# Attention in one encoder kernel: the work of later heads is queued, turn by turn, behind the turn's exponential and negated maximum

## The chip, the cores and the metric

The kernel runs on one core of a Trainium2 chip. A core has engines that each work through a queue of their own and wait for one another by semaphores: TensorE (PE in the profile, with its weight loads as PEld) for matmuls, VectorE (DVE), ScalarE (ACT), GpSimd (POOL) and SyncE (SP, which here only issues DMAs). The metric is device time in microseconds of one execution; a median of several runs stands for a kernel.

## The reference

The program is an encoder trunk of two residual layers on 512 tokens of width 1024, all in float32. Layer 0 mixes tokens with a gated linear attention, layer 1 with softmax attention; each is followed by a gated MLP with a short convolution. The change lies in layer 1's attention alone, which computes

```python
q = apply_rope(rmsnorm(q, q_norm)...)   # 8 heads of 128
k = apply_rope(rmsnorm(k, k_norm)...)   # 2 heads; query heads 0-3 use the first, 4-7 the second
...
s = einsum('bkgqd,bksd->bkgqs', q_blk, k) * scale    # per block of 128 queries
p = softmax(s, axis=-1)
o = einsum('bkgqs,bksd->bkgqd', p, v)
...
return o @ w_out
```

With 512 tokens and blocks of 128 queries there are 4 blocks for each of 8 heads, so 32 blocks. Each has a score tile of 128 queries by 512 keys.

## The kernel before

Products run on TensorE in a reduced float format. To keep precision each operand is split in a high part and a low rest, and a product is three matmuls (`mm3`, lines 253 to 255): high by high, high by low, low by high. So every weight half of 128x1024 has to be made into a pair, `wh` and `wl`. In most of the kernel ACT makes `wh` by a rounding copy (L140) and DVE makes `wl` by a subtraction (L141). In the attention layer DVE is relieved: ACT makes `wh` (L123) and a negated copy in `wl` (L124), and POOL issues a DMA that adds the raw weight into `wl` (L133, called from `flush`). `W.half` returns a pair that has been made and makes the one after it, so a pair is made one call ahead. `wh` and `wl` have three buffers each, the raw weights two of 1 MB, which SP loads.

The attention layer first projects keys, the first pair of query heads and the values. Then comes the loop over turns t = 0 to 37, which the change touches. One turn does, in the order in which the program is traced:

- `scores` of block t: three matmuls into a bank "s" (two banks), the row maximum on DVE (L753), the negated and scaled maximum nb on DVE (L754), the exponential p with its row sum on ACT (L756)
- what the `plan` has for the turn: steps of generators that do work of later heads
- `turn` of block t - 4: four transposes of p on TensorE (L774) into a bank "pt" (two banks), a rounding copy on ACT (L777) and its rest on DVE (L778)
- `shares` of block t: the reciprocal of the sum (L761) and p times it (L762), on DVE
- `mix` of block t - 6, for two blocks at a time: twelve matmuls of the transposed probabilities with the values into bank "po", and for every fourth block the split of the head's result on ACT and DVE (L678, L679).

The plan has two kinds of generators. Three are the query projections `qpair` of the pairs of heads 1 to 3, of 27 steps each: 8 steps of matmuls into a bank A and 8 into a bank B (the three matmuls of one of eight slices each), then squares of A and B on ACT (L642, L643), their sum (L644), four products with the rotary tables on DVE (`turned`, L652), the sums of squares over a head on TensorE (`hs`, L626, into a "pt" bank) with its scale on DVE and POOL (L628, L193, L197, L633), the rotation's sums on POOL (L671, L672), and two splits of the finished q on ACT and DVE (L678, L679). `Q_STEPS` and `Q_READY` say how many steps fall into which turn: pair 1 has its matmuls in turns 0 to 3 and the rest in turns 4 to 8, pair 2 in turns 4 to 10 and 11 to 16, pair 3 in turns 11 to 19 and 20 to 24. Scores of pair i begin with block 8i. The fourth generator is the output projection `out_steps`, with six matmuls a step (L308) in the turns of `O_STEPS`, from turn 22 on; what is left of it follows the loop. The calls of `W.half` fall into turns 0, 2, 4, 7, 11, 15, 22 and 29, and then 32 and 36.

The order on each engine is not the traced order. A scheduler at compile time plays the program through and gives each engine its next instruction from those that are ready, with earlier traced ones first. So an instruction of a generator whose operands are ready early can stand on its engine well ahead of the turn that it was traced in. What follows from data (a value, a buffer to be freed) is kept by semaphores.

Of the kernel before, what the change touches and what calls it, by code (L numbers as in the profile page):

```python
# [11 lines left out]
AF = mybir.ActivationFunctionType  # L12
ALU = mybir.AluOpType
# [33 lines left out]
def hybrid_encoder_kernel(  # L47
# [21 lines left out]
    pe, act, dve, pool, sync = nc.tensor, nc.scalar, nc.vector, nc.gpsimd, nc.sync  # L69
# [14 lines left out]
    def bank(tag, n):  # L84
        return pp.tile([P, S], F32, tag=tag, bufs=PS[tag], name=nm(n))
# [7 lines left out]
    def tmp(tag, n, w=S):  # L93
        return sp.tile([P, w], F32, tag=tag, bufs={"u": 4, "t": 6, "sq": 3}[tag], name=nm(n))

    def tiny(w, n, tag="tiny"):
        return sp.tile([P, 8], F32, tag=tag, bufs={"tiny": 36, "tiny2": 4}[tag], name=nm(n))[:, :w]
# [153 lines left out]
    def mm3(ps, wh, wl, mh, ml, start, stop):  # L251

        mm(ps, wh, mh, start=start, stop=False)  # L253
        mm(ps, wh, ml, start=False, stop=False)  # L254
        mm(ps, wl, mh, start=False, stop=stop)  # L255
# [356 lines left out]
    def attention(norm, nxt):  # L612
# [89 lines left out]
        def qpair(i, tag="acc"):  # L702
            ys, sc = yield from roped(1 + i, PC_QK, HD ** -0.5, "qsc", tag)
            for e in range(2):
                yield
                t = big(F32R, "q")
                split(ys[e], t)
                heads[2 * i + e] = (t, sc, e)
# [35 lines left out]
        def scores(h, j):  # L744

            qt, sc, e = heads[h]
            kt = kk[h // 4]
            js = slice(j * P, (j + 1) * P)
            s = bank("s", "s")
            mm3(s, qt[:, js], qt[:, S + j * P : S + (j + 1) * P], kt[:, :S], kt[:, S:], True, True)  # L750
            scj = sc[:, 2 * j + e : 2 * j + e + 1]
            mx, nb, sm, rc = (tiny(1, n) for n in ("mx", "nb", "sm", "rc"))
            dve.reduce_max(mx, s, axis=mybir.AxisListType.X)  # L753
            dve.tensor_scalar(nb, mx, scj, -1.0, ALU.mult, ALU.mult)  # L754
            p = tmp("t", "p")
            act.activation(p, s, AF.Exp, scale=scj, bias=nb, accum_out=sm)  # L756
            probs[h, j] = (p, sm, rc)

        def shares(h, j):
            p, sm, rc = probs[h, j]  # L760
            dve.reciprocal(rc, sm)  # L761
            dve.tensor_scalar(p, p, rc, None, ALU.mult)  # L762
            probs[h, j] = p

        def turn(h, j):

            hf, i = divmod(j, 2)
            if i == 0:
                pts[h, hf] = tuple(big(F32R, n).rearrange("p (k q) -> p k q", q=256) for n in ("pth", "ptl"))
            ph3, pl3 = pts[h, hf]  # L770
            p = probs.pop((h, j))
            tp = bank("pt", "pt")
            for k in range(NT):
                pe.transpose(tp[:, k * P : (k + 1) * P], p[:, k * P : (k + 1) * P], ident)  # L774
            isl = slice(i * P, (i + 1) * P)
            tp3 = tp.rearrange("p (k q) -> p k q", q=P)
            act.activation(ph3[:, :, isl], tp3, AF.Copy)  # L777
            dve.tensor_tensor(pl3[:, :, isl], tp3, ph3[:, :, isl].bitcast(F32), ALU.subtract)  # L778

        def mix(h, hf):  # L780
            ph3, pl3 = pts.pop((h, hf))
            vo = (h // 4) * HD
            if hf == 0:
                pos[h] = bank("po", "po")
            dst = pos[h][:, hf * 256 : (hf + 1) * 256]
            for k in range(NT):
                vsl = slice(k * 256 + vo, k * 256 + vo + HD)
                mm3(dst, vh[:, vsl], vl[:, vsl], ph3[:, k, :], pl3[:, k, :], k == 0, k == NT - 1)
            if hf == 1:
                t = big(F32R, "oT") if h < 4 else pair("xhl", 8, F32R, "oT")  # L790
                split(pos[h], t)
                oh[h] = (t[:, :S], t[:, S:])

        LAG, LAG2 = LAGS
        blocks = [(h, j) for h in range(QH) for j in range(NT)]
        osteps = out_steps(w_aout, oh, nxt)
        plan = collections.defaultdict(list)
        for i in range(1, QH // 2):
            g = qpair(i)
# [3 lines left out]
        for t in O_STEPS:  # L803
            plan[t].append(osteps)
        for t in range(len(blocks) + LAG2):
            if t < len(blocks):
                scores(*blocks[t])
            for g in plan[t]:
                next(g, None)
            if LAG <= t < len(blocks) + LAG:  # L810
                turn(*blocks[t - LAG])
            if t < len(blocks):
                shares(*blocks[t])
            if t >= LAG2:
                h, j = blocks[t - LAG2]
                if j % 2 == 1:
                    mix(h, j // 2)
# [3 lines left out]
    cw = gla(norms[0], norms[1])  # L821
    ffn(0, norms[1], cw, norms[2])
    attention(norms[2], norms[3])
    ffn(1, norms[3], cw, None)

# [80 lines left out]
```

## Time and profile before

| what | value |
|---|---|
| runs | 1138.2, 1138.27, 1138.65 us; median 1138.27 |
| profiled execution | 1138.36 us, of which the profile's span is 1136.6 |
| TensorE busy | 1128.9 us, 99% of the span, 5280 matmuls |
| DVE, ACT, POOL busy | 688.0, 481.5, 84.4 us |
| granted TensorE clock | 0.999 of full speed |

The span goes from the first to the last instruction of the profile. A row of a timeline gives the start in us from the span's start, the duration in us, the engine, the line, the operation, what it writes and reads with shapes, and in brackets the idle time of the engine before it and what ended it. Matmuls overlap, and the ends of their records are modelled: the step from one matmul's start to the next is what it costs, not the length of its record. In a row of waits stand the total in us, how often, and the longest.

### The profile page before, as it was taken

Reading aid. Unit: us, or ns where it says so; the run is one execution under the profiler, and the core shown is the slowest. Engines: PE = TensorE matmul, PEld = TensorE weight load, DVE = VectorE, ACT = ScalarE, POOL = GpSimd, SP = SyncE. Lnnn points to the kernel's source line nnn. Section 1 sums busy time; section 2 is a strip of 40 time slices with the busy share of each in tenths; the row PEclk is TensorE's granted clock in tenths of the full one; section 3 lists DMA queues with packets and bytes.
Section 4 is the critical chain, followed back from the end, with each engine's and each line's share of the span. In section 5 each row is a group of like instructions: output and inputs, shape, how many; then the busy total and the mean of one; then the engine's idle time right before and its main releaser. Section 6 shows DMA issues by size and latency. Waiting matters only on the chain. (4 is left out here: it accounts for less than half of the span.)

```text
span 1136.6 us, 13040 instructions
## 1 busy us (share of the span) xinstructions
PE 1128.9 (99%) x5280; PEld 941.8 (83%) x5280; DVE 688.0 (61%) x997; ACT 481.5 (42%) x691; POOL 84.4 (7%) x73
## 2 busy tenths in 40 slices
PE   9999999999999999999999999999999999999998
PEld 7788888888888888888888888888888888888887
DVE  5677653567776777633325689756777777762221
ACT  6465233444444444432234666644444444441210
POOL 0214110000000000000004333000000000000000
PEclk9999999999999999999999999999999999999999
DMA  6322211232322323223257632222232322323320
GB/s 229 137 86 74 78 71 38 74 106 80 111 80 106 111 75 111 91 95 112 76 151 182 149 75 74 56 75 94 92 111 75 111 100 86 111 80 124 130 93 19
DMA packets 19980, 111.66 MB, mean 98 GB/s; under 512 B 2384, under 2 KB 3024, under 8 KB 8400
## 3 DMA queue, kind: packets, MB, share of 16 engines
q1 hardware_dynamic: 17328, 102.29, 25.7%
q0 software_dynamic: 2304, 8.39, 3.9%
q8 instruction: 41, 0.67, 0.2%
q10 hardware_dynamic: 288, 0.15, 0.0%
q14 instruction: 19, 0.16, 0.0%
HBM read 100.34 MB, written 2.10 MB: 90 GB/s over the span
## 5 line engine op out<-in xcount | busy, mean ns | idle before, releaser
L140 ACT ACTIVATE wh<-raw 128x1024 fp32r<-128x1024 f32 x164 | 173.0, 1055 | 339.6 <-PE up L254 132.5
L141 DVE TENSOR_TENSOR wl<-raw,wh 128x1024 fp32r<-128x1024 f32 x164 | 203.8, 1243 | 149.9 <-ACT wh L140 149.5
L253 PE MATMUL up<-xhl,wh 128*128 128x512 f32 x704 | 274.3, 390 | 0.0
L255 PE MATMUL up<-xhl,wl 128*128 128x512 f32 x704 | 273.9, 389 | 0.0
L254 PE MATMUL up<-xhl,wh 128*128 128x512 f32 x704 | 273.9, 389 | 0.0
L255 PEld LDWEIGHTS up<-xhl,wl 128*128 128x128 f32 x704 | 132.2, 188 | 27.6
L254 PEld LDWEIGHTS up<-xhl,wh 128*128 128x128 f32 x704 | 132.2, 188 | 27.3
L253 PEld LDWEIGHTS up<-xhl,wh 128*128 128x128 f32 x704 | 132.2, 188 | 27.2
L253 PE MATMUL dn<-gu,wh 128*128 128x512 f32 x352 | 136.9, 389 | 0.0
L254 PE MATMUL dn<-gu,wh 128*128 128x512 f32 x352 | 136.9, 389 | 0.0
L255 PE MATMUL dn<-gu,wl 128*128 128x512 f32 x352 | 136.9, 389 | 0.0
L579 DVE TENSOR_TENSOR u<-up,R 128x512 f32<-128x512 f32 x88 | 60.3, 687 | 52.7 <-PE up L255 52.6
L581 ACT ACTIVATE y<-u,cw 128x512 f32<-128x512 f32 x88 | 71.2, 811 | 21.6 <-DVE u L579 21.6
L254 PEld LDWEIGHTS dn<-gu,wh 128*128 128x128 f32 x352 | 66.1, 188 | 13.8
L253 PEld LDWEIGHTS dn<-gu,wh 128*128 128x128 f32 x352 | 66.1, 188 | 13.7
L255 PEld LDWEIGHTS dn<-gu,wl 128*128 128x128 f32 x352 | 66.1, 188 | 13.6
L308 PE MATMUL op<-oT,wh 128*128 128x512 f32 x256 | 70.6, 394 | 0.0
L583 DVE SCALAR_TENSOR_TENSOR y<-u,cw,y 128x511 f32<-128x511 f32 x88 | 65.9, 751 | 2.9
L582 DVE SCALAR_TENSOR_TENSOR y<-u,cw,y 128x511 f32<-128x511 f32 x88 | 65.5, 746 | 0.6 <-ACT y L581 0.6
L585 ACT ACTIVATE y<-y 128x512 f32<-128x512 f32 x44 | 27.9, 634 | 87.8 <-DVE y L583 87.7
L308 PEld LDWEIGHTS op<-oT,wh 128*128 128x128 f32 x256 | 47.2, 188 | 9.8 <-ACT oT L539 0.3
L282 PE MATMUL vg<-wl,xhl 128*128 128x512 f32 x128 | 49.9, 390 | 0.2 <-DVE wl L141 0.2
(191 smaller groups left out, 1504.8 us busy)
## 6 DMA issues: line engine op xcount, KB each, us to landing
raw<-in_w_up_dram SPq DMA_DIRECT2D x44, 1024.0 KB, 4.7
raw<-in_w_down_dram SPq DMA_DIRECT2D x22, 1024.0 KB, 4.7
wl<-raw POOLq DMA_DIRECT2D x16, 512.0 KB, 4.6
raw<-in_w_vg_dram SPq DMA_DIRECT2D x6, 1024.0 KB, 4.8
raw<-in_w_akq_dram SPq DMA_DIRECT2D x5, 1024.0 KB, 5.2
raw<-in_w_kq_dram SPq DMA_DIRECT2D x4, 1024.0 KB, 4.7
raw<-in_w_gout_dram SPq DMA_DIRECT2D x4, 1024.0 KB, 4.8
raw<-in_w_aout_dram SPq DMA_DIRECT2D x4, 1024.0 KB, 4.8
```

The lines of the kernel that those rows point to most:

```text
L140: act.activation(hi[:, sl], r[:, sl], AF.Copy)
L141: dve.tensor_tensor(lo[:, sl], r[:, sl], hi[:, sl].bitcast(F32), ALU.subtract)
L253: mm(ps, wh, mh, start=start, stop=False)
L254: mm(ps, wh, ml, start=False, stop=False)
L255: mm(ps, wl, mh, start=False, stop=stop)
L282: mm(ps[j][:, :width], xh, wl[:, sl], start=False, stop=False)
L308: mm(pss[ng][n], wt[:, sl], mv, start=k == 0 and i == 0, stop=k == KC - 1 and i == 2)
L579: dve.tensor_tensor(u, ps, norm.R, ALU.mult)
L581: act.activation(y, u, AF.Identity, scale=w(1), bias=w(3))
L582: dve.scalar_tensor_tensor(y[:, 1:], u[:, : S - 1], w(0), y[:, 1:], ALU.mult, ALU.add)
L583: dve.scalar_tensor_tensor(y[:, : S - 1], u[:, 1:], w(2), y[:, : S - 1], ALU.mult, ALU.add)
L585: act.activation(res[1], res[1], AF.Silu)
```

## The change

`scores` now returns two instructions: nb's (the last that it puts on DVE) and the exponential (on ACT). The loop opens `tc.issue_after` for both around the turn's planned steps. Within the block, each instruction that is traced on the engine of the given one gets an ordering edge to it: the scheduler may not place it on that engine before the given one. It is an edge of issue order on one engine alone, with no semaphore and no wait for the given instruction's end. So in turn t planned instructions on DVE stand behind nb of block t, planned instructions on ACT behind exponential t. Instructions of TensorE, POOL and SP get no edge. `turn`, `shares` and `mix` stay outside the block; from turn 32 on there are no scores and no edges.

```diff
             dve.reduce_max(mx, s, axis=mybir.AxisListType.X)
-            dve.tensor_scalar(nb, mx, scj, -1.0, ALU.mult, ALU.mult)
+            last = dve.tensor_scalar(nb, mx, scj, -1.0, ALU.mult, ALU.mult)
             p = tmp("t", "p")
-            act.activation(p, s, AF.Exp, scale=scj, bias=nb, accum_out=sm)
             probs[h, j] = (p, sm, rc)
+            return last, act.activation(p, s, AF.Exp, scale=scj, bias=nb, accum_out=sm)
...
         for t in range(len(blocks) + LAG2):
-            if t < len(blocks):
-                scores(*blocks[t])
-            for g in plan[t]:
-                next(g, None)
+            with ExitStack() as behind:
+                if t < len(blocks):
+                    for i in scores(*blocks[t]):
+                        behind.enter_context(tc.issue_after(i.ins))
+                for g in plan[t]:
+                    next(g, None)
             if LAG <= t < len(blocks) + LAG:
```

## The prediction

> **What bounds the kernel now.** I read the page first: engine totals, then the chain that ended last.
>
> ```profile
> span 1136.6 us, 13040 instructions
> PE 1128.9 (99%) x5280; PEld 941.8 (83%) x5280; DVE 688.0 (61%) x997; ACT 481.5 (42%) x691; POOL 84.4 (7%) x73
> ...
> PE 37%; ACT 0%; POOL 0%; DVE 0%; DVEq 0%; issue 0%
> ```
>
> TensorE is busy for 1128.9 of 1136.6 us and is the only engine on the chain with a share. So a stretch in which TensorE finds nothing to do is added to the time whole, and no other engine's saving counts unless it feeds TensorE. Next the windows: the loop over the 32 blocks, from the first scores at 629 to the last at 727, and its 18 us tail. The columns are busy times of PE, weight load, DVE, ACT and POOL, then clock, DMA share and GB/s.
>
> ```profile
> 629.00:727.00 98.00, 96.92 (x558) 82.12 (x558) 78.34 (x189) 66.29 (x125) 29.75 (x25) 1.00 0.39 93
> 727.00:745.00 18.00, 18.00 (x112) 15.63 (x111) 8.41 (x17) 6.42 (x12) 0.00 (x0) 1.00 0.12 52
> ```
>
> The loop holds 98.00 - 96.92 = 1.08 us of idle TensorE. No more than that can be gained there, but for waits that overlapping records hide. The waits of the stretch 620 to 750 (total, times, longest):
>
> ```profile
> ACT p L756 <- DVE nb L754: 17.0, 17, 2.6
> PEld s L253 <- ACT p L756: 2.3, 5, 1.0
> PE s L253 <- ACT p L756: 0.8, 1, 0.8
> ```
>
> ACT sits before the exponential for 17.0 us, waiting for the negated maximum, and this costs TensorE at most the other two lines: 2.3 us of weight loads that waited for a scores bank, 0.8 of them visible on TensorE itself. The rest of the time other work keeps TensorE fed: the projection of later heads (A, B) and the output projection (op). That other work is what the change touches.
>
> **The change part by part.** No instruction is added or taken away. In turn t, what the planned generators issue on ACT must now stand behind exponential t (L756) in ACT's queue, and what they issue on DVE behind nb t (L754). TensorE, POOL and SP are not bound, except through data. The planned ACT work is of two kinds: squares and splits of q, and the making of weight halves: wh (L123) and wl (L124), after which POOL issues an accumulating DMA into wl (L133). Each call for a half makes the next one, so the halves are made in turns 0, 2, 4, 7, 11, 15, 22 and 29, and the last, in turn 32, meets no exponential. Where they stand today, in the timeline of ACT:
>
> ```profile
> 625.93 1.04 ACT L123 ACTIVATE wh<-raw 128x1024 fp32r<-128x1024 f32 x1
> 626.88 1.04 ACT L124 ACTIVATE wl<-raw 128x1024 fp32r<-128x1024 f32 x1
> ...
> 629.76 1.06 ACT L123 ACTIVATE wh<-raw 128x1024 fp32r<-128x1024 f32 x1
> ...
> 634.48 0.78 ACT L756 ACTIVATE p<-s,nb,qsc 128x512 f32<-128x512 f32 x1 [1.41 <-DVE nb L754]
> 635.15 0.19 ACT L756 ACTIVATION_READ_ACCUMULATOR p<-s,nb,qsc 128x1 f32 x1
> 636.68 0.78 ACT L756 ACTIVATE p<-s,nb,qsc 128x512 f32<-128x512 f32 x1 [1.34 <-DVE nb L754]
> ...
> 639.82 0.78 ACT L756 ACTIVATE p<-s,nb,qsc 128x512 f32<-128x512 f32 x1
> ...
> 695.08 1.05 ACT L123 ACTIVATE wh<-raw 128x1024 fp32r<-128x1024 f32 x1
> ...
> 725.55 0.77 ACT L756 ACTIVATE p<-s,nb,qsc 128x512 f32<-128x512 f32 x1
> 726.21 0.20 ACT L756 ACTIVATION_READ_ACCUMULATOR p<-s,nb,qsc 128x1 f32 x1
> 726.30 0.60 ACT L777 ACTIVATE pth<-pt 128x512 fp32r<-128x512 f32 x1
> ...
> 727.80 0.78 ACT L756 ACTIVATE p<-s,nb,qsc 128x512 f32<-128x512 f32 x1 [0.91 <-DVE nb L754]
> ```
>
> Counting halves in the order of their use, 625.93 is the second half of head pair 1 (turn 0), 629.76 the first half of pair 2 (turn 2) and 695.08 the third half of the output weights (turn 29). The exponentials of turns 0, 2 and 29 stand at 634.48, 639.82 and 725.55. All eight makings run ahead of their exponential today, so the change binds: by about 9 us in the first case and 30 us in the last. What matters is when TensorE wants them.
>
> ```profile
> 637.64 0.39 PE L253 MATMUL B<-xhl,wh 128*128 128x512 f32 x1
> ...
> 638.10 0.39 PE L255 MATMUL B<-xhl,wl 128*128 128x512 f32 x1
> ...
> 640.36 0.39 PE L253 MATMUL s<-k,q 128*128 128x512 f32 x1
> ...
> 641.04 0.39 PE L253 MATMUL B<-xhl,wh 128*128 128x512 f32 x1
> ...
> 644.90 0.39 PE L255 MATMUL A<-xhl,wl 128*128 128x512 f32 x1
> 646.11 1.05 PE L626 MATMUL hs<-bd,qa 128*128 128x2 f32 x8
> ...
> 647.58 0.60 PE L774 MATMUL pt<-ident,p 128*128 128x128 f32 x4
> ```
>
> ```profile
> 628.22 0.87 POOL L133 DMA_DIRECT2D wl<-raw  x1 [2.86 <-ACT wl L124]
> ```
>
> ```profile
> wl<-raw POOLq DMA_DIRECT2D x16, 512.0 KB, 4.6
> ```
>
> **Term 1, the second half of pair 1.** Exponential 0 cannot come earlier, as it waits for DVE's nb. Its accumulator read ends at 635.34; wh starts 0.1 before that (neighbouring ACT rows overlap by as much), at 635.2, and wl 0.95 later (626.88 - 625.93), at 636.2, ending at 637.2. POOL issues 0.3 after wl's end (627.92 to 628.22), so at 637.5, and the data land 4.6 later, at 642.1. TensorE first wants wl at 638.10: 4.0 us are open. Cover: scores of blocks 3 and 4, each 0.68 us (640.36 to 641.04), once exponentials 1 and 2 have freed their two banks; that is 1.4. The transposes of blocks 0 to 2 would cover more, but in turn 4 the plan draws a "pt" bank for hs before the first transpose draws one, and today hs (646.11) does stand ahead of the first pt (647.58). hs needs all of B. I estimate that they cannot go ahead, and take 4.0 - 1.4 = 2.6. The bounds are 0 (transposes and a mix also go ahead) and 4.0 (no cover, if the blocked matmul stands in TensorE's queue ahead of the scores).
>
> **Pair 2 and the halves between.** Pair 2's first half would follow exponential 2, by the same offsets: wh at 640.6, wl's end at 642.6, the DMA from 642.9 to 647.5, against a wish at 644.90, which term 1 moves to 647.5. That comes out level: 0. The halves of turns 4 to 22 are wanted three to seven turns later; a turn is about 98/32 = 3.1 us, and making takes 2.0 + 0.3 + 4.6 = 6.9. I take 0, with TensorE's other planned work as the cover; if one misses, it costs part of a turn, up to 1.
>
> **Term 2, the third half of the output weights.** It is made in turn 29 and wanted in turn 32.
>
> ```profile
> 730.06 0.63 PE L308 MATMUL op<-oT,wh 128*128 128x512 f32 x2
> 730.53 0.40 PE L308 MATMUL op<-oT,wl 128*128 128x512 f32 x1
> ...
> 733.52 0.60 PE L774 MATMUL pt<-ident,p 128*128 128x128 f32 x4
> 733.88 0.36 PE L253 MATMUL po<-pth,vh 128*128 128x256 f32 x1
> ...
> 735.39 1.09 PE L308 MATMUL op<-oT,wh 128*128 128x512 f32 x4
> ```
>
> After exponential 29, wh and wl end between 728.3 (both at once) and 729.6 (split by L777 at 726.30 and exponential 30 at 727.80). With 0.3 and 4.6 the data are there between 733.2 and 734.5; the wish is at 730.53, so 3.4 us are open in the middle. Cover: four transposes of 0.36 (733.52 to 733.88) and two mixes of 1.51 (733.88 to 735.39), 4.4 in all, but each waits for ACT and DVE copies of the one before, so I count half, 2.1. I take 1.3; the bounds are 0 and 4.0.
>
> **Term 3, the wait that goes.** The single visible stall is at block 24's scores:
>
> ```profile
> 709.04 0.50 PE L253 MATMUL s<-k,q 128*128 128x512 f32 x1 [0.80 <-ACT p L756]
> ```
>
> ```profile
> 705.27 1.14 DVE L762 TENSOR_SCALAR p<-p,rc 128x512 f32<-128x512 f32 x1
> ```
>
> Exponential 22 was late there because DVE was full; one share of p took 1.14 us. With planned DVE work behind nb this may go, but part of DVE's work there (shares, transposed copies) is not planned. I take -0.5, between 0 and -1.1 (all idle of the loop). Next to be late is the q split of pair 3, now in turns 23 and 24; TensorE has output steps as cover.
>
> **The DVE part.** Turning of q and its low half move behind nb. They must be done before scores of the next pair; the rows of ACT waiting 17.0 us for nb show that nb comes late in a turn, so these products end about a turn later than today. Cover is again planned matmul work, cost 0; without it part of the 1 us above.
>
> **Sum.** 2.6 + 0 + 1.3 - 0.5 = 3.4 us. The profiled execution took 1138.36 (span 1136.6 and 1.76 around it), 0.09 over the median of the runs, 1138.27. So 1138.27 + 3.4 = 1141.7. About 0.2%, 2.3 us, is what a measurement of this kernel can tell from no change: slower begins at 1140.5, faster ends at 1136.0.
>
> **The rivals.** *Covered:* the scheduler pulls transposes and a mix of the first blocks under term 1 (up to three times 0.36 and one 1.51 more, which brings 2.6 to 0) and enough of the tail under term 2. Time between 1137.2 and 1140.5, middle 1138.6. For it: p of block 0 exists long before its transpose at 647.58. Against: hs ahead of it. *Exposed:* TensorE's queue has the blocked matmul ahead of the scores and the tail's op ahead of the transposes: 4.0 + 4.0 + up to 1 gives 1146 to 1147. For it: the queue is set at compile time, so a landing that is placed too early there stalls everything behind. Against: today's order left one stall only. *Faster:* the exponential coming first frees scores banks, and all 2.3 us of weight-load wait go while the halves arrive in time: 1136.0. It decides only if both open gaps (4.0 and 3.4) are covered whole. *No effect:* excluded, since all eight makings run ahead of their exponential today.
>
> *A quicker landing:* the accumulating DMA of a half lands in about 3 us where it is alone on its queue, and terms 1 and 2 shrink to 1.2 and 0. That gives 1138.27 + 0.7 = 1139.0. The smallest of 16 landings is far above it:
>
> ```profile
> DMA to landing us min/median/max: 4.5/4.6/7.0
> ```
>
> The Trainium skill, "DMA: Bandwidth & Descriptors", section "Anatomy of one DMA — SWDGE (gpsimd) path", has a POOL-issued DMA at about 2.0 us plus its bytes over 436 GB/s; for 512 KB that is an estimate of 3.2 us. The trace does not agree (4.5 at least), and the measured row stands in the sum.
>
> **How the numbers follow.** Main case 0.52 (1140.5 to 1143.9), covered 0.26, exposed 0.14, faster 0.06, quicker landing 0.02. Slower: 0.52 + 0.14 = 0.66; same: 0.28; faster: 0.06. The range 1138.0 to 1145.5 leaves out faster, the lowest part of covered and the top of exposed, together near 0.2. The main case's own range is 1140.5 to 1143.9.
>
> **What would show it.** In the changed trace: wh of pair 1's second half behind exponential 0, near 635; its DMA near 637.5; the first L255 of B near 642 with idle TensorE before it; the tail's making behind exponential 29, with idle TensorE near 731 to 735; block 24's stall gone or smaller. Transposes ahead of hs, or B's first wl matmul without idle time before it, would prove term 1 wrong; a stall before scores of a new pair would mean that the DVE part was not covered.

## The result

The changed kernel takes 1156.39 us (median of five runs, 1154.51 to 1159.38) where the kernel before takes 1138.27. The ratio is 1.0159, with a 95% interval of 1.0140 to 1.0178: 18.1 us slower. The direction was forecast. The amount was not: 3.4 us were forecast, and the range ended at 1145.5. The five runs differ in the granted clock of TensorE: 0.997 in the two at 1154.5, 0.994 in the three from 1156.39 up.

The profiled execution of the changed kernel took 1157.54 us, 19.2 more than the profiled one of before (1138.36). Its page begins with the same number of instructions, and the chain that ended last has new members:

```profile
span 1155.8 us, 13040 instructions
...
PE 1137.3 (98%) x5280; PEld 946.2 (82%) x5280; DVE 687.4 (59%) x997; ACT 480.9 (42%) x691; POOL 84.1 (7%) x73
...
PE 91%; issue 3%; DVE 2%; DMA 2%; POOL 1%; ACT 1%; SPq 0%; DVEq 0%; POOLq 0%; ACTq 0%
```

TensorE's busy time itself has grown, from 1128.9 to 1137.3 us, with the same 5280 matmuls. Idle time grew by about 11 us (1155.8 - 1137.3 against 1136.6 - 1128.9). So there are two losses to explain: TensorE waits longer, and it runs slower.

The windows of the changed trace (busy PE, weight load, DVE, ACT, POOL, then granted clock, DMA share and GB/s) say where. The scores of the last block start at 743.1 us instead of 726.5.

```profile
629.00:650.00 21.00, 17.12 (x80) 13.28 (x78) 9.96 (x29) 13.45 (x23) 3.67 (x4) 1.00 0.43 94
650.00:661.00 11.00, 9.10 (x28) 7.73 (x29) 2.92 (x7) 1.46 (x3) 2.27 (x2) 0.53 0.58 155
661.00:710.00 49.00, 48.34 (x284) 40.92 (x283) 38.50 (x91) 30.45 (x58) 14.80 (x12) 1.00 0.24 55
710.00:751.00 41.00, 35.69 (x210) 29.12 (x209) 31.39 (x76) 26.18 (x51) 9.50 (x8) 0.98 0.25 59
751.00:754.00 3.00, 3.00 (x13) 2.39 (x13) 0.00 (x0) 0.00 (x0) 0.00 (x0) 0.70 0.56 97
```

Before 661 and after 710 TensorE is idle for several us where it had 1.08 in the whole loop. In the second window, 650 to 661, its granted clock is 0.53: 28 matmul records fall into 11 us. The waits of TensorE from 620 to 770 (total, times, longest):

```profile
PE A L255 <- DMA wl<-raw: 3.6, 1, 3.6
PE op L308 <- DMA wl<-raw: 2.2, 2, 1.2
PE pt L774 <- DVE ptl L778: 1.8, 3, 1.1
PE s L253 <- ACT q L678: 1.3, 2, 0.7
PE s L253 <- ACT p L757: 1.2, 1, 1.2
PE B L255 <- DMA wl<-raw: 0.9, 1, 0.9
```

In before, the only such line on TensorE was the 0.8 us wait for p. The largest wait here belongs to a projection of head pair 2, a place that the prediction had at zero. The exponential of turn 0 with the half that is made behind it, and the half behind the exponential of turn 2, from ACT's timeline:

```profile
634.88 0.78 ACT L757 ACTIVATE p<-s,nb,qsc 128x512 f32<-128x512 f32 x1 [3.30 <-DVE nb L754]
...
635.65 1.05 ACT L123 ACTIVATE wh<-raw 128x1024 fp32r<-128x1024 f32 x1
...
640.51 1.05 ACT L123 ACTIVATE wh<-raw 128x1024 fp32r<-128x1024 f32 x1
```

The pair's making stands directly behind the exponential, 635.65 against the 635.2 of the forecast. From there on, TensorE, POOL and SP:

```profile
638.49 0.46 PE L253 MATMUL s<-k,q 128*128 128x512 f32 x1
...
640.66 0.50 PE L253 MATMUL s<-k,q 128*128 128x512 f32 x1 [1.24 <-ACT p L757]
...
642.54 0.50 PE L255 MATMUL B<-xhl,wl 128*128 128x512 f32 x1 [0.91 <-DMA wl<-raw]
...
647.89 0.39 PE L254 MATMUL A<-xhl,wh 128*128 128x512 f32 x1
651.90 0.80 PE L255 MATMUL A<-xhl,wl 128*128 128x512 f32 x1 [3.63 <-DMA wl<-raw]
652.50 0.63 PE L253 MATMUL A<-xhl,wh 128*128 128x512 f32 x1
652.92 0.63 PE L254 MATMUL A<-xhl,wh 128*128 128x512 f32 x1
```

```profile
637.94 0.91 POOL L133 DMA_DIRECT2D wl<-raw  x1 [3.55 <-ACT wl L124]
642.80 0.85 POOL L133 DMA_DIRECT2D wl<-raw  x1 [3.94 <-ACT wl L124]
```

```profile
642.63 0.33 SPq L118 DMA_DIRECT2D raw<-in_w_akq_dram  x1
```

```profile
DMA to landing us min/median/max: 4.5/4.6/9.1
```

The last fence is the time from issue to landing of all sixteen such DMAs. Up to 642.80 everything is as forecast, within 0.5 us. But the DMA of 642.80 brings the low half that TensorE needs at 648.1, and TensorE gets it at 651.9. It is the one that took 9.1 us. Just before its issue, at 642.63, SP starts a load of 1 MB of raw weights. The reason for that moment is in the buffers: the load's target has held the raw weights of pair 1, and comes free when pair 1's own accumulating DMA has landed, at 642.5. After the stall, the steps between matmuls show the slow clock: 652.50 to 652.92 is 0.42 us, where the same step takes 0.23 at full clock (the last matmul before the stall, at 647.89, started 0.23 after the one ahead of it).

### The profile page after: what moved, and what is told of

Its sections match the earlier page's. It is cut to its first block, busy times and chain, and to the rows that moved or that the text cites. A ratio compares the mean times of both kernels' runs of the same rounds, so it can differ in the third digit from the quotient of the medians.

```text
span 1155.8 us, 13040 instructions
## 1 busy us (share of the span) xinstructions
PE 1137.3 (98%) x5280; PEld 946.2 (82%) x5280; DVE 687.4 (59%) x997; ACT 480.9 (42%) x691; POOL 84.1 (7%) x73
## 4 chain that ended last, share of the span: by engine, by line
PE 91%; issue 3%; DVE 2%; DMA 2%; POOL 1%; ACT 1%; SPq 0%; DVEq 0%; POOLq 0%; ACTq 0%
PE up L253 14%; PE up L255 14%; PE up L254 14%; PE op L308 7%; PE dn L253 7%; PE dn L255 7%; PE dn L254 7%; PE vg L282 2%; PE vg L283 2%; PE vg L281 2%; PE o L524 1%; DMA wl<-raw 1%; PE kv L503 1%; PE pt L774 1%; PE k L255 1%
```

## The experiments

Two theories stood at the start. W: the loss comes from the weight halves, whose way from ACT's making over POOL's DMA to TensorE takes 6.9 us and now begins an exponential too late. R: it comes from the rotary work of the next head pair (squares, products, splits), which comes late for its scores. Later runs take the front of the loop, the landing, the clock and the order of TensorE apart. The kernel before was run beside each batch, with medians from 1138.20 to 1138.57.

### Which engine's edge: e1_dve and e2_act

```diff
-                    for i in scores(*blocks[t]):
+                    for i in scores(*blocks[t])[:1]:    # e1_dve: the edge behind nb alone
+                    for i in scores(*blocks[t])[1:]:    # e2_act: the edge behind the exponential alone
```

> Only DVE's planned work is queued behind nb; ACT's planned work is free as before. Theory W (the loss comes from weight halves that ACT makes too late): the weights are early again, so 1136.5 to 1140, within 0.2% of before, and no slow clock in the loop. Rival R (the loss comes from the rotary work of later heads, which reaches the scores late): its DVE half is queued as in the changed kernel, so at least half of the 18 us stays, 1147 to 1156.

> Only ACT's planned work is queued behind the exponential; DVE's is free as before. Theory W: the whole loss stays, 1153 to 1160, with the wait of A's third matmul near 648 to 652 and half clock after it. Rival R: the DVE products are early again, so less than half of the loss stays, 1139 to 1147.

With DVE's edge alone the kernel takes 1140.13 us, 1.75 over before by medians (ratio 1.0010, 1.0002 to 1.0019): 0.13 over the range of theory W, and far from that of R. Four of the sixteen runs of the kernel before in that batch took 1140.1 to 1140.7 too, so these 1.75 us are rough. With ACT's edge alone it takes 1157.49, ratio 1.0164 (1.0150 to 1.0178), which is all of the loss. So ACT's queue is the place, and it carries both kinds of work: weight halves, and squares and splits of q.

### Which work on ACT: e3_weights and e4_rest

Here the edges are set by name: behind the turn's nb and exponential only the two instructions that make a weight half (e3), or everything but those (e4).

```diff
-                act.activation(hi, r, AF.Copy)
-                act.activation(lo, r, AF.Copy, scale=-1.0)
+                for made in (act.activation(hi, r, AF.Copy), act.activation(lo, r, AF.Copy, scale=-1.0)):
+                    making.add(made.ins.name)
...
-                        behind.enter_context(tc.issue_after(i.ins))
+                        behind.enter_context(queue_behind(i.ins, lambda i: i.name in making))      # e3_weights
+                        behind.enter_context(queue_behind(i.ins, lambda i: i.name not in making))  # e4_rest
```

> Of the planned work only the two activations that make a weight half (wh and wl) are queued behind the exponential; squares, splits of q and all DVE work are free. Theory W: 1152 to 1160. Rival R: 1137 to 1142.

> The complement: all planned work on ACT and DVE is queued as in the changed kernel, except the two activations that make a weight half. Theory W: 1136.5 to 1141. Rival R: 1150 to 1158.

The weights alone cost 12.8 us: 1151.18, ratio 1.0103 (1.0086 to 1.0121). All the rest alone costs 3.6: 1141.93, ratio 1.0029 (1.0018 to 1.0041). Both miss the ranges of W by about 0.9 us, and those of R by 8 us and more. The waits of e4 are short ones, the longest 0.6 us. W holds for the larger part, and R as the main cause falls. The parts are not independent: together these two give 16.4 of the 18.1, while the squares and splits, put behind the exponential beside the weights, add 6.3 (e2 less e3). Both figures are rough, as e3's runs stand in two groups: 1149.1 with a granted clock of 0.997 to 0.998, and 1153.2 with 0.994.

### Which turns: e7_from3 and e8_first3

The halves of turns 0 and 2 are those of the front, the rest come later.

```diff
-                        behind.enter_context(tc.issue_after(i.ins))
+                        if t >= 3:    # e7_from3
+                        if t < 3:     # e8_first3
+                            behind.enter_context(tc.issue_after(i.ins))
```

> The edges of turns 0, 1 and 2 are left out, all later ones stay. Theory W in two places: the front (pair 1's second half, pair 2's first half, and the slow clock after them) is some 10.5 us of the loss, the rest in the later turns some 7.5. So 1144.5 to 1147.5 here. If the front alone carried the loss: 1138 to 1140.

> The complement: edges in turns 0, 1 and 2 alone. Theory W in two places: 1147.5 to 1150.5, with both waits at the front and the slow clock after them, and none in the tail. If the later turns carried the loss: 1138 to 1141.

Edges in turns 0 to 2 alone: 1147.91, ratio 1.0082 (1.0066 to 1.0098), 9.3 us. From turn 3 on: 1147.71, ratio 1.0087 (1.0069 to 1.0105), 9.1 us, 0.2 over its range. They add up to 18.4, the whole loss. In e8 the same wait stands at the same place, and the clock falls there too, but for 3.4 us only (651.08 to 654.49); in the profile of the changed kernel it was 10.2 us. The tail (730 to 750) is clean:

```profile
651.61 0.80 PE L255 MATMUL A<-xhl,wl 128*128 128x512 f32 x1 [3.54 <-DMA wl<-raw]
```

```profile
651.08:654.49 3.41, 2.88 (x7) 2.30 (x8) 0.98 (x2) 0.54 (x1) 0.86 (x1) 0.50 0.95 187
...
730.00:750.00 20.00, 19.99 (x124) 17.08 (x124) 13.39 (x29) 10.02 (x20) 0.41 (x1) 1.00 0.29 79
```

Of the 9.1 us of the later turns, e4's 3.6 are work that is not weights, if that work costs in the first three turns nothing; the other 5.5 would be the halves. That split is a difference of two runs, not measured by itself.

### The raw load beside the accumulating DMA: e5_raw_later

This run leaves the orders on TensorE, ACT and POOL as they are after the change, adds one small instruction on DVE, and only makes the 1 MB raw load of pair 3 wait for that instruction, a memset that is traced in turn 5. The load then starts after pair 2's low half has landed.

```diff
+        def early(self, src):
+            t = sp.tile([P, 4 * S], F32, tag="raw", bufs=2, name=nm("raw"))
+            dve.memset(t[:, :8], 0.0)
+            sync.dma_start(t, src[0])
+            self.raw[id(src), 0] = t
...
+                if t == 5:
+                    W.early(qk_order[4])
```

> The changed kernel with one transfer later: the 1 MB load of pair 3's raw weights waits for a small DVE write that is traced in turn 5, so it no longer starts beside the accumulating DMA of pair 2's first half. Queue orders of TensorE, ACT and POOL stay. Theory C (that DMA lands 9.1 us after its issue because the load shares the 16 engines with it): it lands in 4.6, the 3.6 us wait of A's third matmul falls to below 0.5, TensorE keeps full clock there, and the time falls by 7 to 9 us, to 1147 to 1150. Rival (the landing is late for another reason, as POOL or the queue): the wait and the half clock stay, 1154 to 1159.

It takes 1150.20, ratio 1.0106 (1.0088 to 1.0124), at the upper end of its range, 6.2 us less than the changed kernel by the medians; the two profiled executions differ by 9.9 (1147.69 and 1157.54). The load starts at 653.17, the wait before pair 2's low half is gone, and so is the slow clock:

```profile
653.17 0.33 SPq L133 DMA_DIRECT2D raw<-in_w_akq_dram  x1
```

```profile
647.70 0.39 PE L261 MATMUL A<-xhl,wl 128*128 128x512 f32 x1
```

```profile
650.00:670.00 20.00, 20.00 (x115) 16.80 (x115) 16.13 (x38) 11.41 (x22) 8.09 (x7) 1.00 0.56 158
```

The landing of pair 2's DMA alone, in the window 642 to 643 in which POOL issues it:

```profile
DMA to landing us min/median/max: 4.5/4.5/4.5
```

So the load made the landing late: 9.1 us with it, 4.5 without. The half is there when it is wanted, at 647.70, which is what the prediction had assumed (landing at 647.5). The other runs of this kernel, 1149.6 to 1151.8, have mean granted clocks from 0.996 to 0.998 where the profiled one has 1.0: they lose something to the clock that the trace does not show. And the profile of the changed kernel is of a run with 0.994, so the 9.9 us hold a long slow stretch on one side and none on the other.

### The clock: e6_filler

Sixteen useless matmuls into a spare bank stand where TensorE waits for pair 2's low half. They add work and end no wait earlier; if the slow clock comes from the idle time, the kernel must become faster.

```diff
+            if k == 0 and filler:
+                mm(ps, wh[:, sl], hl[k][0], start=True, stop=False)
+                mm(ps, wh[:, sl], hl[k][1], start=False, stop=False)
+                spare = bank("po", "fill")
+                for n in range(filler):
+                    mm(spare, wh[:, sl], hl[k][0], start=n == 0, stop=n == filler - 1)
+                mm(ps, wl[:, sl], hl[k][0], start=False, stop=False)
```

> The changed kernel with 16 matmuls of 0.23 us without use (into a spare bank, their result is not read) put into TensorE's queue where it waits for pair 2's first half. The data come as late as before. Theory H (idle TensorE loses half of its clock for some 9 us): the wait's end stays at about 652, the slow stretch after it goes, and the time falls by 3.5 to 4.5 us, to 1151.5 to 1153.5, though TensorE does 3.6 us more work. Rival (the slow stretch has nothing to do with the idle time): 1156 to 1160.

It takes 1151.69, ratio 1.0117 (1.0101 to 1.0133), 4.7 us less than the changed kernel, with 16 more matmuls. The DMA still takes 8.8 us, and the needed half is used at 652.31, 0.4 later than without the filler. But the matmuls from there on run at full rate, 0.23 us apart:

```profile
647.73 1.75 PE L266 MATMUL fill<-xhl,wh 128*128 128x512 f32 x7
649.32 0.95 PE L634 MATMUL hs<-bd,qa 128*128 128x2 f32 x8
650.13 2.34 PE L266 MATMUL fill<-xhl,wh 128*128 128x512 f32 x9
652.31 0.39 PE L267 MATMUL A<-xhl,wl 128*128 128x512 f32 x1
652.54 0.39 PE L253 MATMUL A<-xhl,wh 128*128 128x512 f32 x1
```

The filler let hs be placed ahead of seven matmuls of A that it had followed, so its own gain is not of the clock alone; hs takes about 0.8 us (649.32 to 650.13), which bounds that part. The rest of the 4.7 is clock (0.999 or 1.0 in all four runs, against 0.994 to 0.997), though not of this stretch alone: the profile of e6 has no slow stretch in the tail either, where that of the changed kernel has a short one.

### The order of TensorE in term 1: e9_hs_bank

The prediction rested on hs holding back the transposes by its "pt" bank. Here pair 1's hs draws from "po".

```diff
-            ps = bank("pt", "hs")
+            ps = bank(tag, "hs")
...
-            r = scale_tok(qa)
+            r = scale_tok(qa, "po" if i == 2 else "pt")
```

> The changed kernel with pair 1's hs in the po bank instead of a pt bank. Theory P (the transposes of the first blocks cannot cover the wait because hs, which needs all of B, draws its pt bank first): two groups of transposes, 0.36 us each, now run within the first idle time between 639 and 642.5, the idle time there falls from 2.2 to 1.4 or 1.5, and the time by 0.5 to 1.5 us, to 1154.5 to 1157, within the spread of the slow clock. Rival (p is not ready so early): they run, but wait, and the idle time stays at 2.2.

Eight transposes now go ahead, at 639.08, and the wait for p shrinks from 1.24 to 0.31 us. The other two waits stay:

```profile
639.08 1.09 PE L774 MATMUL pt<-ident,p 128*128 128x128 f32 x8
...
640.48 0.50 PE L253 MATMUL s<-k,q 128*128 128x512 f32 x1 [0.31 <-ACT p L757]
...
642.35 0.50 PE L255 MATMUL B<-xhl,wl 128*128 128x512 f32 x1 [0.91 <-DMA wl<-raw]
...
651.55 0.58 PE L255 MATMUL A<-xhl,wl 128*128 128x512 f32 x1 [3.46 <-DMA wl<-raw]
```

The time is 1155.22, ratio 1.0151 (1.0133 to 1.0169), 1.2 less than the changed kernel by medians, with overlapping intervals. The reason given for the order was right, and 0.9 us of idle time is what it is worth at this place. The time does not confirm that figure: in e9's profile the waits of scores for the split of q have grown from 1.3 to 2.9 us, and the slow stretch after A's wait lasts 3.4 us (651.83 to 655.25) instead of 10.2.

### The lead of the DMA: e10_dve_low

The low parts of pairs 1 and 2 are made by DVE's subtraction, as in the rest of the kernel, instead of ACT's negated copy and POOL's DMA. The making stays behind the exponential.

```diff
-    W.by_dma += [(a, 1) for a in qk_order + [w_av]] + [(w_aout, 2)]
+    W.by_dma += [(a, 1) for n, a in enumerate(qk_order) if n not in (2, 3)] + [(w_av, 1), (w_aout, 2)]
```

> The changed kernel with the low parts of pairs 1 and 2 made by a DVE subtraction instead of ACT's negated copy and the accumulating DMA; all edges stay. Theory L (what the edges expose is the 6.9 us that a half takes from exponential to landing, of which the DMA is 4.9): a half is ready some 2.5 us after its exponential, so both waits at the front go, and the time is that of the run with edges from turn 3 on, 1145 to 1149. Rival (the two activations on ACT are too late whatever follows them): at least 1 us of idle time stays at each of the two places, 1150 to 1156.

It takes 1148.58, ratio 1.0089 (1.0073 to 1.0105): 7.8 us less than the changed kernel, and about the time of e7, which has no edges in the front at all. The front is clean, and pair 1's low half is used at 638.41, 0.3 after the 638.10 of before:

```profile
638.41 0.39 PE L255 MATMUL B<-xhl,wl 128*128 128x512 f32 x1
```

```profile
629.00:650.00 21.00, 20.78 (x102) 17.21 (x101) 13.04 (x32) 10.64 (x20) 1.67 (x1) 1.00 0.15 50
```

So it is not the place behind the exponential that costs the front, but the lead of about 6.9 us that a half with a DMA needs after it, and for pair 2 the late landing, which goes with the DMA. None of these versions is faster than the kernel before.

## Why the prediction was wrong, and where it was right

**What bounds the kernel** was right: TensorE's idle time went into the total whole. What was missing is that idle time also has a second price, the clock, so that one us of idle TensorE can cost more than one us.

**The change binds** was right: the halves of turns 0 and 2 are made directly behind their exponentials, at 635.65 and 640.51.

**Term 1** (2.6 us) was right, with its mechanism: two scores were pulled ahead (638.49 and 640.66), the first low matmul of B came at 642.54 (forecast 642), and the idle time in front was 1.24 + 0.91 = 2.15 us. Half of it stands before the second score instead of before B, because that score waits for its bank. e9 shows that hs held the transposes back, as argued.

**Pair 2 "comes out level: 0"** is the step that failed. The issue at 642.80 was forecast at 642.9. The landing was taken at 4.6 us, the median of sixteen, and was 9.1. The row of the prediction that showed 4.6 also showed a largest landing of 7.0, and it was never asked which DMAs the long ones were. They are those beside a raw load: in before four of the sixteen took over 6 us (7.0, 6.7, 6.6 and 6.1), each issued 0.7 to 1.7 us after a raw load, and the others 4.5 to 5.0. In before the same load starts at 632.86, pair 2's DMA at 633.96, and the landing of that one DMA (window 633.5 to 636) is the third row:

```profile
632.86 0.33 SPq L118 DMA_DIRECT2D raw<-in_w_akq_dram  x1
```

```profile
633.96 0.90 POOL L133 DMA_DIRECT2D wl<-raw  x1
```

```profile
DMA to landing us min/median/max: 6.6/6.6/6.6
```

The two already ran beside each other there, 11 us before TensorE wanted the half (644.90), so that it did not show. The change moves both together, as the load waits for the raw buffer of pair 1, and so for pair 1's DMA, and pair 2's DMA is issued 0.2 us later. The prediction said that SP is not bound "except through data"; this buffer is that data, and its transfer was not followed. e5 shows the cause: with the load moved alone, the wait is gone.

**The clock** was no term at all, and no rival. In the profile of the changed kernel TensorE is idle from 648.28, after 2.15 us of idle time between 639 and 643. The rows below are windows: the granted clock (third figure from the right) goes to half at 650.40, is still half when TensorE goes on at 651.90, and is full again from 660.64.

```profile
648.28:650.40 2.12, 0.00 (x0) 0.00 (x0) 0.69 (x1) 1.18 (x2) 0.65 (x1) 1.00 0.95 199
650.40:651.90 1.50, 0.00 (x0) 0.00 (x0) 0.00 (x0) 0.00 (x0) 0.21 (x1) 0.50 0.84 161
651.90:660.64 8.74, 8.74 (x27) 7.42 (x28) 2.56 (x7) 1.23 (x2) 1.66 (x1) 0.50 0.55 161
```

At a step of 0.42 instead of 0.23 us, these 8.7 us hold about 4.0 us of loss. e6, where the idle time is filled, takes back 4.7, with hs and the tail in it. Front of the loop in sum, in this profile: 2.15 + 3.63 + 4.0 = 9.8. The size of the last term is not fixed. In e8 the same waits (1.24, 0.91 and 3.54) are followed by 2.88 us of work at half clock, about 1.3 us of loss by the same steps. That makes 7.0 of the 8.6 us by which its profiled execution (1146.91) is over that of before; the rest is not settled. So the 9.3 us of e8's median confirm that the front costs about half of the loss, and not the 9.8 term by term.

**"The halves between": 0, up to 1.** As 0 this was too low, through one half, which costs 0.99 us, about the 1 that had been named as the bound, and through the rotary work. The second half of the output weights is made behind exponential 22, and that exponential is itself late, at 721.83 against 708.13 in before:

```profile
721.83 0.78 ACT L757 ACTIVATE p<-s,nb,qsc 128x512 f32<-128x512 f32 x1 [1.50 <-DVE nb L754]
...
722.60 1.04 ACT L123 ACTIVATE wh<-raw 128x1024 fp32r<-128x1024 f32 x1
```

Its DMA goes out at 724.89, and the output step waits 0.99 us for it:

```profile
725.92 0.50 PE L253 MATMUL s<-k,q 128*128 128x512 f32 x1 [0.68 <-ACT q L678]
...
729.48 0.73 PE L308 MATMUL op<-oT,wl 128*128 128x512 f32 x2 [0.99 <-DMA wl<-raw]
...
749.69 0.79 PE L308 MATMUL op<-oT,wl 128*128 128x512 f32 x1 [1.20 <-DMA wl<-raw]
```

**Term 2** (1.3 us) was right in place: 1.20 us at 749.69, before the third half of the output weights. The cover cost more than was counted: another 1.12 us of idle time stands 2 us earlier (747.62), where a transpose waits for ptl, the low part of the transposed copy, on DVE, so the gap is 2.3 in all. A second, short fall of the clock follows (0.5 from 749.39 to 752.80, of which TensorE works 3.1 us, about 1.4 of loss by the same steps).

**Term 3** (-0.5 us) was wrong. The 0.80 us stall at block 24 is gone, but its first scores now wait 0.68 us for the split of q (725.92, above). The prediction had named that split as next to be late, and then counted output steps as its cover, which were not enough.

**The DVE part: 0** was too low, by little: e1 is 1.75 us over before by medians, and its interval says 0.2 to 2.2. The sign that the prediction had named for this, a stall before scores of a new pair, is there in e1: 1.38 us before those of block 24, for an exponential (0.80 in before), and 0.33 among those of block 8, for the low part of q. The stall at 725.92 is no such sign: e2, with no edge on DVE, has it too (0.68).

For the later turns, e7's own profile is the measure. Its waits before matmuls come to 6.4 us (op's halves 2.2, q 1.9, ptl 1.8, others 0.5) against 0.8 in before, at full clock. That is 5.6 of the 7.7 us by which its profiled execution (1146.06) is over that of before. The other 2.1 are not settled. Its other runs, up to 1150.44, show granted clocks of 0.997 to 0.999, so there the clock costs something too.

Of the rivals, **Exposed** (1146 to 1147) came nearest. Its reason, a landing that TensorE's fixed order takes too early so that all behind it stands still, is what happened, but at pair 2 and not at the two places where its 4.0 were counted: there two scores did go ahead. **Covered** and **Faster** needed the gaps to be filled, and 2.15 and 1.20 us stayed open. **Quicker landing** fell: the smallest landing is again 4.5 us, and the largest grew.

What stays open: at which amount of idle time, in which stretch, the clock falls, and why it stays low for 3.4 us after one wait and for 10.2 after an equal one; and how the loss of the later turns divides between halves and rotary work, which is known only as a difference of runs.

## What to carry to other kernels

An operand that goes through a DMA has to be made its whole way ahead of its use (here 6.9 us: two copies, the issue and the landing), and an edge that ties its making to a late instruction takes this lead away; e10, with a making that has no DMA, pays nothing for the same edge in the front. When a transfer is moved, look up which other transfer its end sets free, and take the landing from a row in which the two run side by side, not from the median. And where TensorE is the bound, price an idle stretch of a few us with what follows it, as the clock may fall: here 3.5 to 3.6 us of waiting cost from 1.3 us (e8) to 4.0 us (the changed kernel) more.

## What the runs showed of the hardware

In the profile of the changed kernel the granted clock of TensorE fell to half 2.1 us into the wait of 3.63, and stayed there for 8.7 us more of work after it. After the same wait the slow stretch lasted 3.4 us in all in e8 and in e9, and in e9 (3.46 us of waiting) it began 0.3 us after TensorE had gone on. So the same wait does not cost the same in every run. In e2, whose first two idle spells were 1.24 and 0.92 us, the clock fell already before the long wait: 0.50 from 642.62 to 646.03, and again from 652.86 to 659.68.

```profile
638.00:643.00 5.00, 2.88 (x12) 1.59 (x10) 2.54 (x8) 3.66 (x8) 0.91 (x1) 0.96 0.56 105
643.00:650.00 7.00, 6.96 (x24) 5.47 (x24) 3.24 (x8) 3.26 (x8) 0.85 (x1) 0.78 0.81 189
```

The Trainium skill, "TensorE: Matmul & The Clock Gate", section "Part 1: The HAM clock gate (the "warmup" mystery)", has the clock go to half after an idle window of about 3.4 us that runs freely, and back after about as long of busy time. The trace agrees on the half rate, and a window that runs on its own would let the same kernel fall at one time and not at another; no run here shows the window itself. It does not agree on the idle time: the clock fell after 2.1 us of the wait, and in e2 after two spells shorter than that. On the way back, 3.4 us of slow clock in e8 and e9 agree, and 8.7 us of work in the changed kernel do not. There the small hs matmuls and the transposes fall into the slow stretch (655.06 to 657.37), in e8 they come after it (from 655.11); whether that matters, no run tests.

An accumulating DMA of 512 KB from POOL landed in 4.5 us when it was alone (e5), in 6.6 beside a 1 MB load that had started 1.1 us earlier (before), and in 9.1 beside one that had started 0.17 us earlier (the changed kernel). The Trainium skill, "DMA: Bandwidth & Descriptors", section "SWDGE vs HWDGE vs iDMA", says that DMAs issued by POOL and by SP use different queues inside each DMA engine, which takes turns between them. That fits a transfer of 4.5 us that takes twice as long; the runs show the two times, not the turns.
